# All four output-projection chunks ahead of the MLP: moving a half's norm and operand sums beside other matrix products

## The chip, the cores and the metric

The kernel runs on 1 core of one Trainium2 chip. The metric is the device time of one execution in microseconds; before the change it is 2526.63 us (median of 3 runs, 2519.16 to 2531.45). Five engines work side by side, each in the order of its own instruction queue: TensorE (PE; its weight loads are shown as PEld), VectorE (DVE), ScalarE (ACT), GpSimd (POOL) and SyncE (SP), which here only issues transfers.

## The reference

One decoder layer on 2048 tokens of width 1024, in float32. The normalised input goes through one combined projection into three head groups (a convolution, a retention and a dilated attention). Their outputs are joined into `mix`. What the change touches is all that follows:

```
mix = concatenate([conv_out, ret_out, att_out], axis=-1) @ w_out     # 1024 x 1024
x   = x + mix
h2  = rms_norm(x, norm2_g)
ff  = square(relu(h2 @ w_ff1)) @ w_ff2                               # 1024 -> 4096 -> 1024
out = x + ff
```

## The kernel before

Everything after attention is held transposed: 128 channels on the partitions, tokens along the free axis. The 2048 tokens are worked in two halves H of 1024, each half in two chunks c of 512. Chunks are written (H,c) here: (0,0), (0,1), (1,0), (1,1). Every float32 operand is split in two parts that TensorE takes: a rounded one (a copy on ACT) and the rest (a subtraction on DVE); `halves` (L616) does both. A product then takes three matmuls per 128 x 128 block (`mm3`, L915).

For each half the stages come one after the other:

1. Output projection. For both chunks and each of 8 blocks d of 128 output channels: load and split a weight block (`woraw`, `wohi`, `wolo`, L636), 24 matmuls into one bank `psc`, add the residual on DVE (L976), store the sum to DRAM from POOL's queue (L977), square it on ACT, add the squares into `ssum` on POOL (L983). In the last four blocks of a chunk the `mix` tiles of the next one are loaded and split. Weights and mix tiles come through the pool `stage`, which has 3 buffers; split weights lie in `wcp`, room for 3 blocks.
2. Norm and sums. `norm_sums` (4 small products `pm`), a power on POOL, `norm_rows` (4 small products `pr`), then the multiplications by `pr`. The up projection takes seven products of 512 x 512 x 128 where eight would be plain, on sums of the two chunks: B11 and B21 (from chunk 0 alone), T1, T2, T3, T4 and B22 (from both). `act_sums` (L1006) makes those sums from the 8 tiles `x1`, and `halves` splits them. Chunk 0 of a half is normalised beside the products of chunk 1; chunk 1 and the sums come after chunk 1's last product.
3. Up projection. 16 pairs of 128 hidden channels, each seven products of 12 matmuls (banks `psx`, `psy`, `psz`). Since the sums are late, the first FIRST = 3 pairs begin with the two products that need only B11 and B21.
4. Down projection. 8 groups g of 4 hidden blocks: load hidden rows and weights, split, 192 matmuls into `pso`, add into `acc` on DVE. In half 0's last group, half 1's first `mix` tiles are loaded; its output projection follows.

The order on each engine is made by a scheduler that simulates the program from its order in the source and from the buffers that are free; the pool `ur` has 24 buffers of 4 KB per partition, for operands and for hidden rows, `ul` 8 and `actp` 8.

Of the kernel before, what the change touches and what calls it, by code (L numbers as in the profile page):

```python
# [48 lines left out]
def kernel(ctx, tc, x, xT, w_in, g1, g2, conv_w, conv_b, conv_g, ret_g, qk_g,  # L49
# [871 lines left out]

    for H in range(2):

        x1 = []
        ssum = [tp.tile([P, CH], F32, tag="ssum", name=f"ssum{c}") for c in range(2)]
        ops = {}

        def norm_sums(c):
            pm = bank("pm2")
            for q in range(4):  # L930
                mm = nc.tensor.matmul(pm[:, q:q + 1], ssum[c][:, q * P:(q + 1) * P], ones[:], start=True, stop=True)
            ms = small.tile([P, 4], F32, tag="ms4", name="ms4")
            nc.vector.tensor_scalar(out=ms[:], in0=pm[:, 0:4], scalar1=1.0 / D, scalar2=EPS,
                                    op0=ALU.mult, op1=ALU.add)
            r2 = small.tile([P, 4], F32, tag="r2", name="r2")
            rsqrt(r2[:], ms[:], 4)
            return r2, mm

        def norm_rows(r2):
            pr = bank("pr2")  # L940
            for q in range(4):
                mm = nc.tensor.matmul(pr[:, q * P:(q + 1) * P], r2[:, q:q + 1].to_broadcast([P, P]), ident[:],
                                      start=True, stop=True)
            return pr, mm

        def after(ins):
            return tc.issue_after(ins.ins) if ins is not None else nullcontext()

        def op_b(name, kp, raw):
            u = unit4(ul, "v", name) if name in ("T1", "T4") else unit4(ur, "u", name)  # L950
            halves(raw, u)
            ops[name, kp] = u

        def load_mix1(k):
            u = unit4(ur, "u", f"mix{k}")
            raw = stage.tile([P, CH], F32, tag="raw", name="mixraw")
            nc.sync.dma_start(out=raw[:], in_=mix_d[k][H][:, CH:2 * CH])
            halves(raw[:], u)
            return u

        for d in range(KT):
            xt = unit4(ur, "u", f"x1_{d}", F32)
            nc.sync.dma_start(out=xt[:], in_=xT[d * P:(d + 1) * P, H * HALF:(H + 1) * HALF]
                              .rearrange("p (c t) -> p c t", c=2))
            x1.append(xt)
        mixes = [mix0 + [load_mix(7, 0, 0, actp)], []] if H == 0 else [mix0, []]
        for c in range(2):
            cs = slice(c * CH, (c + 1) * CH)
            mix = mixes[c]
            for d in range(KT):  # L970
                wo = wout0[d] if H == 0 and c == 0 and d < len(wout0) else load_wout(d)
                xt = x1[d]
                ps = bank("psc")
                for k in range(KT):
                    mm3(ps[:], (wo[0][:, k, :], wo[1][:, k, :]), hl(mix[k]), k == 0, k == KT - 1)
                nc.vector.tensor_tensor(out=xt[:, c, :], in0=xt[:, c, :], in1=ps[:], op=ALU.add)  # L976
                nc.gpsimd.dma_start(out=x1_d[d][:, cs], in_=xt[:, c, :])  # L977
                if d == 0:
                    nc.scalar.activation(out=ssum[c][:], in_=xt[:, c, :], func=AF.Square)
                else:  # L980
                    sq = tp.tile([P, CH], F32, tag="sq", name="sq2", bufs=1)
                    nc.scalar.activation(out=sq[:], in_=xt[:, c, :], func=AF.Square)
                    nc.gpsimd.tensor_tensor(out=ssum[c][:], in0=ssum[c][:], in1=sq[:], op=ALU.add)  # L983
                if H == 0 and c == 0 and d == LATE:
                    while todo:
                        tick()
                    late.close()
                    ul = ctx.enter_context(tc.tile_pool(name="ul", bufs=LAST, reuse_waits="tile"))
                if c == 0 and d >= 4:
                    mixes[1] += [load_mix1(2 * d - 8), load_mix1(2 * d - 7)]  # L990
                if c == 1:
                    nc.scalar.activation(out=xt[:, 1, :], in_=xt[:, 1, :], func=AF.Copy, scale=g2t[:, d:d + 1])
                if c == 1 and d == 1:
                    pr = norm_rows(norm_sums(0)[0])[0]
                    for k in range(KT):
                        nc.vector.scalar_tensor_tensor(out=x1[k][:, 0, :], in0=x1[k][:, 0, :], scalar=g2t[:, k:k + 1],
                                                       in1=pr[:], op0=ALU.mult, op1=ALU.mult)
                    for kp in range(4):
                        op_b("B11", kp, x1[kp][:, 0, :])
                        op_b("B21", kp, x1[kp + 4][:, 0, :])  # L1000
# [224 lines left out]
```

## Time and profile before

| | |
|---|---|
| median of 3 runs | 2526.63 us |
| profiled execution | 2526.32 us, span 2524.5 us |
| PE busy | 2451.7 us, 97% of the span |
| DVE, ACT, POOL busy | 59%, 35%, 21% |
| mean granted clock | 0.978 |

The span runs from the first to the last instruction. Busy shares are means over stages that differ; "granted clock" is the share of full speed that TensorE was given, and its two levels are 1.2 and 2.4 GHz. A window of the trace counts an instruction that crosses its edge on both sides. Half 0's output projection begins at 921.8 us, half 1's ends at 1825.5 us.

### The profile page before, as it was taken

Reading aid. Unit: us, or ns where it says so; the run is one execution under the profiler, and the core shown is the slowest. Engines: PE = TensorE matmul, PEld = TensorE weight load, DVE = VectorE, ACT = ScalarE, POOL = GpSimd, SP = SyncE. Lnnn points to the kernel's source line nnn. Section 1 sums busy time; section 2 is a strip of 40 time slices with the busy share of each in tenths; the row PEclk is TensorE's granted clock in tenths of the full one; section 3 lists DMA queues with packets and bytes.
Section 4 is the critical chain, followed back from the end, with each engine's and each line's share of the span. In section 5 each row is a group of like instructions: output and inputs, shape, how many; then the busy total and the mean of one; then the engine's idle time right before and its main releaser. Section 6 shows DMA issues by size and latency. Waiting matters only on the chain.

```text
span 2524.5 us, 32832 instructions
## 1 busy us (share of the span) xinstructions
PE 2451.7 (97%) x12062; PEld 2027.7 (80%) x12062; DVE 1483.5 (59%) x2864; ACT 884.9 (35%) x2005; POOL 537.9 (21%) x387
## 2 busy tenths in 40 slices
PE   7999999999999989899999999999989999999999
PEld 6878889999878767668888888888768888888887
DVE  5576787763486765785556545444586556654542
ACT  6433325333566564432223212112432223221210
POOL 0231212232142323642320000001553222000000
PEclk9999999999898899989999999999989999999999
DMA  7312104432353437222236323245422223632311
GB/s 222 122 63 72 43 14 118 114 95 81 101 114 76 106 103 255 88 100 109 100 111 224 132 79 122 67 160 181 143 73 110 109 109 119 222 122 71 117 67 67
DMA packets 189997, 284.19 MB, mean 113 GB/s; under 512 B 40093, under 2 KB 129292, under 8 KB 189836
## 3 DMA queue, kind: packets, MB, share of 16 engines
q1 hardware_dynamic: 187276, 273.70, 33.6%
q0 software_dynamic: 2560, 8.39, 0.9%
q8 instruction: 95, 1.56, 0.3%
q14 instruction: 66, 0.54, 0.1%
HBM read 210.04 MB, written 71.99 MB: 112 GB/s over the span
## 4 chain that ended last, share of the span: by engine, by line
PE 84%; DVE 6%; DMA 6%; ACT 2%; issue 1%; SPq 1%; POOL 0%; ACTq 0%; DVEq 0%; POOLq 0%
PE pso L917 28%; PE ps L158 15%; PE psy L917 11%; PE psz L917 7%; PE psx L917 6%; PE psc L917 5%; PE po L712 2%; PE pt L691 2%; PE sp L665 2%; DMA xn<-x 2%; PE sp L666 2%; DVE T L619 1%; PE rsp L350 1%; DMA woraw<-w_out 1%; PE rpo L365 1%
## 5 line engine op out<-in xcount | busy, mean ns | idle before, releaser
L917 PE MATMUL pso<-hid,w2a 128*128 128x512 f32 x1536 | 361.3, 396 | 0.0
L917 PE MATMUL pso<-hid,w2b 128*128 128x512 f32 x1536 | 361.0, 396 | 0.0
L1004 DVE TENSOR_TENSOR acc<-acc,pso 128x512 f32<-128x512 f32 x256 | 175.2, 685 | 296.0 <-PE pso L917 295.2
L917 PEld LDWEIGHTS pso<-hid,w2b 128*128 128x128 f32 x1536 | 288.6, 188 | 69.8
L917 PEld LDWEIGHTS pso<-hid,w2a 128*128 128x128 f32 x1536 | 288.6, 188 | 69.8
L158 PE MATMUL ps<-whi,hh 128*128 128x384 f32 (+1 forms) x896 | 313.5, 351 | 13.6 <-ACT whi L117 9.6
L158 PE MATMUL ps<-whi,hl 128*128 128x384 f32 (+1 forms) x896 | 315.0, 352 | 0.0
L158 PE MATMUL ps<-wlo,hh 128*128 128x384 f32 (+1 forms) x896 | 311.8, 348 | 0.0
L917 PE MATMUL psy<-T,S 128*128 128x512 f32 x768 | 203.3, 412 | 7.8 <-DVE T L619 5.5
L917 PE MATMUL psx<-B,A 128*128 128x512 f32 x768 | 191.2, 396 | 0.0
L158 PEld LDWEIGHTS ps<-whi,hh 128*128 128x128 f32 x896 | 169.5, 189 | 25.4 <-ACT whi L117 9.6
L917 PEld LDWEIGHTS psy<-T,S 128*128 128x128 f32 x768 | 149.6, 196 | 49.3 <-DVE T L619 10.3
L158 PEld LDWEIGHTS ps<-whi,hl 128*128 128x128 f32 x896 | 169.3, 189 | 11.3 <-issue 5.4
L158 PEld LDWEIGHTS ps<-wlo,hh 128*128 128x128 f32 x896 | 169.3, 189 | 9.6 <-issue 3.1
L217 DVE SCALAR_TENSOR_TENSOR acc<-cbuf,cwt,acc 128x512 f32<-128x512 f32 x240 | 175.5, 776 | 0.2
L917 PEld LDWEIGHTS psx<-B,A 128*128 128x128 f32 x768 | 144.0, 188 | 34.3
L1004 POOL TENSOR_TENSOR s<-w1raw 128x512 f32<-128x512 f32 x64 | 91.0, 1439 | 354.9 <-DMA w1raw<-w_ff 318.9
L917 PE MATMUL psc<-mix,wohi 128*128 128x512 f32 x512 | 163.1, 398 | 3.0 <-DVE ml L673 2.1
L619 DVE TENSOR_TENSOR S<-s,S 128x512 fp32r<-128x512 f32 x128 | 107.4, 843 | 68.8 <-ACT S L617 68.2
L676 ACT ACTIVATE lt<-lt,ml 128x256 f32<-128x256 f32 (+1 forms) x288 | 129.3, 452 | 29.9 <-DVE ml L673 29.3
L617 ACT ACTIVATE S<-s 128x512 fp32r<-128x512 f32 x128 | 80.0, 628 | 157.7 <-PE psy L917 94.1
L617 ACT ACTIVATE w2b<-w2raw 128x512 fp32r<-128x512 f32 x64 | 40.1, 626 | 260.2 <-DVE acc L1004 233.0
(192 smaller groups left out, 4011.8 us busy)
## 6 DMA issues: line engine op xcount, KB each, us to landing
w1raw<-w_ff SPq DMA_DIRECT2D x68, 512.0 KB, 3.3
hidraw<-hid_d SPq DMA_DIRECT2D x64, 512.0 KB, 4.2
w2raw<-w_ff SPq DMA_DIRECT2D x64, 512.0 KB, 4.0
woraw<-w_out SPq DMA_DIRECT2D x33, 512.0 KB, 4.0
hid_d<-hidB SPq DMA_DIRECT2D x32, 512.0 KB, 2.6
hid_d<-hidA SPq DMA_DIRECT2D x32, 512.0 KB, 2.6
xs<-xT SPq DMA_DIRECT2D x31, 512.0 KB, 3.9
qkraw<-qkT_d SPq DMA_DIRECT2D x48, 256.0 KB, 4.8
```

Of the source, the lines that this page charges most:

```text
L158: nc.tensor.matmul(ps, a[:, k, :], b[k][:], start=(k == 0 and m == 0), stop=(k == KT - 1 and m == 2))
L217: nc.vector.scalar_tensor_tensor(out=accs[j], in0=src, scalar=cwt[:, j, w:w + 1], in1=accs[j], op0=ALU.mult, op1=ALU.add)
L350: nc.tensor.matmul(sp[:, :w], kT[0:n, a, :], qm[0:n, h0:h1, :], start=True, stop=True)
L617: nc.scalar.activation(out=u[:, 0, :], in_=raw, func=AF.Copy)
L619: sub.tensor_tensor(out=u[:, 1, :], in0=raw, in1=u[:, 0, :].bitcast(F32), op=ALU.subtract)
L665: nc.tensor.matmul(sp[:, c0:c0 + n], qs[h][:, qsl], khi[h][:, ksl], start=True, stop=False)
L666: nc.tensor.matmul(sp[:, c0:c0 + n], qs[h][:, qsl], klo[h][:, ksl], start=False, stop=True)
L676: last_exp[0] = nc.scalar.activation(out=lt[:, :n], in_=lt[:, :n], func=AF.Exp, scale=-1.0, bias=mls[u][:, h:h + 1], accum_out=mls[u][:, 2 ...
L691: nc.tensor.transpose(pts[u][:, q * P:(q + 1) * P], lts[h, u][:, c * P:(c + 1) * P], ident[:])
L712: nc.tensor.matmul(po[h * 64:(h + 1) * 64, u0 * P:(u0 + n) * P], vt[:, kv, h * 64:(h + 1) * 64], mv, start=(one or i == 0), stop=(one or i ...
L917: nc.tensor.matmul(ps, w[a], act[b], start=(first and m == 0), stop=(last and m == 2), skip_group_check=more)
L1004: eng.tensor_tensor(out=out, in0=a, in1=b, op=op)
```

## The change

`out_chunk(H, c, mix, steps)` is now a function, and it runs four times, for (0,0), (0,1), (1,0) and (1,1), ahead of the first up projection. `steps` gives what the source places behind a block d. Norm and sums of half 0 stand beside the chunks of half 1. The residual sums of half 1 pass through 8 rotating tiles of `ul`, are stored to DRAM, and are loaded again into `x1` in half 0's down projection (group 5, block 7); their norm, left operands and sums stand beside half 0's last two groups or behind them. All sums and norm multiplications of chunk 1 are on DVE (12 operations per half were on POOL), the ACT scaling by g2 is gone, and FIRST is 2. The seven products, the down projection and the number of matmuls are as before.

```diff
-FIRST = 3
+FIRST = 2
+    def act_sums(H, kp):
+        lo, hi = x1[H, kp], x1[H, kp + 4]
+        tt(nc.vector, lo[:, 0, :], lo[:, 1, :], lo[:, 0, :], ALU.subtract)
+        t = ur.tile([P, CH], F32, tag="u", name="t2")
+        tt(nc.vector, t[:], hi[:, 1, :], lo[:, 0, :], ALU.subtract)
+        op_b("T2", kp, t[:])
+        tt(nc.vector, lo[:, 1, :], hi[:, 1, :], lo[:, 1, :], ALU.subtract)
+        tt(nc.vector, hi[:, 0, :], hi[:, 0, :], t[:], ALU.subtract)
...
+    def out_chunk(H, c, mix, steps):
+        cs = slice(c * CH, (c + 1) * CH)
+        for d in range(KT):
+            wo = wout0[d] if H == 0 and c == 0 and d < len(wout0) else load_wout(d)
+            if H == 0:
+                xt = x1[0, d][:, c, :]
+            else:
+                xt = ul.tile([P, CH], F32, tag="v", name="x1")
+                nc.sync.dma_start(out=xt[:], in_=xT[d * P:(d + 1) * P, HALF + c * CH:HALF + (c + 1) * CH])
+                xt = xt[:]
+            ps = bank("psc")
+            for k in range(KT):
+                mm3(ps[:], (wo[0][:, k, :], wo[1][:, k, :]), hl(mix[k]), k == 0, k == KT - 1)
+            tt(nc.vector, xt, xt, ps[:], ALU.add)
+            nc.gpsimd.dma_start(out=x1_d[H][d][:, cs], in_=xt)
...
+            for step in steps.get(d, ()):
+                step()
...
+    out_chunk(0, 1, mixes[1], {1: [lambda: norm_sums(0, 0)], 2: [lambda: normalise(0, 0)],
+                               **{d: [more(2, 2 * d - 8, ur), more(2, 2 * d - 7, ur)] for d in range(4, 8)}})
+    out_chunk(1, 0, mixes[2], {0: [lambda: norm_sums(0, 1)], 1: [lambda: normalise(0, 1)], 3: [lambda: left_ops(0)],
+                               **{d: [more(3, 2 * d - 8, actp), more(3, 2 * d - 7, actp)] for d in range(4, 8)}})
+    out_chunk(1, 1, mixes[3], {0: [lambda: norm_sums(1, 0)], **{kp + 1: [lambda kp=kp: act_sums(0, kp)]
+                                                               for kp in range(4)},
+                               5: [lambda: right_ops(0, ("T3", "T1"))]})
+    right_ops(0, ("T4", "B22"))
...
+            if H == 0 and j == 0:
+                norm_sums(1, 1)
...
+        def load_next():
+            for d in range(KT):
+                x1[1, d] = unit4(ur, "u", f"x1_{d}", F32)
+                nc.sync.dma_start(out=x1[1, d][:], in_=x1_d[1][d][:].rearrange("p (c t) -> p c t", c=2))
...
+        next_half = {(end - 3, 7): [load_next], (end - 2, 1): [lambda: normalise(1, 0)],
+                     (end - 2, 4): [lambda: normalise(1, 1)], (end - 1, 0): [lambda: left_ops(1)]}
+        for g in range(end):
+            group(g)
+        if H == 0:
+            sums_next()
+            right_ops(1, ("T3", "T1", "T4", "B22"))
```

How this moves instructions is seen at three places. First PE's queue from half 0's last output-projection block into the up projection, before (a row is one 128 x 512 block with its count; `psx` takes the products with B11 and B21, `pm` and `pr` are the small products of the norm):

```order
L917 MATMUL psx<-B_10525,A_10766 128x512 x3
L931 MATMUL pm_10782<-ones,ssum_9988 128x1 x4
L917 MATMUL psx<-B_10507,A_10796 128x512 x3
L917 MATMUL psx<-B_10513,A_10796 128x512 x3
L917 MATMUL psx<-B_10519,A_10796 128x512 x3
L917 MATMUL psx<-B_10525,A_10796 128x512 x3
L917 MATMUL psx<-B_10510,A_10812 128x512 x3
L917 MATMUL psx<-B_10516,A_10812 128x512 x3
L917 MATMUL psx<-B_10522,A_10812 128x512 x3
L917 MATMUL psx<-B_10528,A_10812 128x512 x3
L942 MATMUL pr_10828<-ident,r_10789 128x128 x4
L917 MATMUL psx<-B_10507,A_10928 128x512 x3
```

and now, behind the last block of chunk (1,1):

```order
L917 MATMUL psc<-mix_11152,wolo 128x512
L917 MATMUL psx<-B_10941,A_11561 128x512 x3
L917 MATMUL psx<-B_10947,A_11561 128x512 x3
L917 MATMUL psx<-B_10953,A_11561 128x512 x3
L917 MATMUL psx<-B_10959,A_11561 128x512 x3
L917 MATMUL psx<-B_10941,A_11582 128x512 x3
L917 MATMUL psx<-B_10947,A_11582 128x512 x3
L917 MATMUL psx<-B_10953,A_11582 128x512 x3
L917 MATMUL psx<-B_10959,A_11582 128x512 x3
L917 MATMUL psy<-T_11243,S_11631 128x512 x3
L917 MATMUL psy<-T_11289,S_11631 128x512 x3
L917 MATMUL psy<-T_11335,S_11631 128x512 x3
```

The norm's small products have left this place, and the first product on a sum (T2, tiles T_11243 and on, into `psy`) follows two products with B11.

Second, DVE's queue behind block 1 of half 1's first chunk, before (`wolo` is the rest part of a weight block, `mix` that of a mix tile, `x<-x,psc` the residual add):

```order
L976 TENSOR_TENSOR x_1_15337<-x_1_15337,psc 128x512
L642 TENSOR_TENSOR wolo<-woraw,wohi 128x1024
L619 TENSOR_TENSOR mix_15575<-mixraw,mix_15575 128x512
L619 TENSOR_TENSOR mix_15580<-mixraw,mix_15580 128x512
L976 TENSOR_TENSOR x_2_15339<-x_2_15339,psc 128x512
L642 TENSOR_TENSOR wolo<-woraw,wohi 128x1024
L619 TENSOR_TENSOR mix_15621<-mixraw,mix_15621 128x512
L619 TENSOR_TENSOR mix_15626<-mixraw,mix_15626 128x512
L976 TENSOR_TENSOR x_3_15341<-x_3_15341,psc 128x512
```

and now, from the weight split behind that block's residual add on:

```order
L642 TENSOR_TENSOR wolo<-woraw,wohi 128x1024
L619 TENSOR_TENSOR mix_11051<-mixraw,mix_11051 128x512
L950 SCALAR_TENSOR_TENSOR x_0_9996<-x_0_9996,g2t,pr_10852 128x512
L950 SCALAR_TENSOR_TENSOR x_1_9998<-x_1_9998,g2t,pr_10852 128x512
L950 SCALAR_TENSOR_TENSOR x_2_10000<-x_2_10000,g2t,pr_10852 128x512
```

then four more of the eight multiplications with `pr`, and the rest of the rows up to the next weight split:

```order
L950 SCALAR_TENSOR_TENSOR x_7_10010<-x_7_10010,g2t,pr_10852 128x512
L929 TENSOR_TENSOR x_0_9996<-x_0_9996 128x512
L619 TENSOR_TENSOR mix_11056<-mixraw,mix_11056 128x512
L929 TENSOR_TENSOR x_1_9998<-x_1_9998 128x512
L929 TENSOR_TENSOR x_2_10000<-x_2_10000 128x512
L929 TENSOR_TENSOR x_10871<-x_10871,psc 128x512
L929 TENSOR_TENSOR x_3_10002<-x_3_10002 128x512
L642 TENSOR_TENSOR wolo<-woraw,wohi 128x1024
```

Half 0's second norm and the first subtractions of its sums have come between two weight splits of half 1.

Third, DVE's queue where half 1's sums are made, before (behind the half's last output-projection block):

```order
L1004 TENSOR_TENSOR x_0_15335<-x_0_15335,pr_16092 128x512
L1004 TENSOR_TENSOR x_1_15337<-x_1_15337,pr_16092 128x512
L1004 TENSOR_TENSOR x_2_15339<-x_2_15339,pr_16092 128x512
L1004 TENSOR_TENSOR x_3_15341<-x_3_15341,pr_16092 128x512
L1004 TENSOR_TENSOR x_0_15335<-x_0_15335 128x512
L1004 TENSOR_TENSOR x_1_15337<-x_1_15337 128x512
L1004 TENSOR_TENSOR x_2_15339<-x_2_15339 128x512
L1004 TENSOR_TENSOR x_3_15341<-x_3_15341 128x512
L619 TENSOR_TENSOR A_16290<-w1raw,A_16290 128x512
L1004 TENSOR_TENSOR t_16111<-x_4_15343,x_0_15335 128x512
L619 TENSOR_TENSOR T_16151<-x_0_15335,T_16151 128x512
```

and now, in the last group of half 0's down projection (acc_13668 is its block d = 7, added to once per chunk):

```order
L929 TENSOR_TENSOR acc_13666<-acc_13666,pso 128x512 x2
L929 TENSOR_TENSOR t_16057<-x_4_15378,x_0_15370 128x512
L929 TENSOR_TENSOR x_4_15378<-x_4_15378,t_16057 128x512
L929 TENSOR_TENSOR t_16065<-x_5_15380,x_1_15372 128x512
L619 TENSOR_TENSOR T_16059<-t_16057,T_16059 128x512
L929 TENSOR_TENSOR acc_13668<-acc_13668,pso 128x512
L929 TENSOR_TENSOR x_5_15380<-x_5_15380,t_16065 128x512
L619 TENSOR_TENSOR T_16112<-x_4_15378,T_16112 128x512
```

The differences between the two chunks and the splits of T1 now stand ahead of these rows, beside the last group's products; the tiles `t` and T of T2 come when that group's hidden rows free their buffers.

## Rows read from the trace of the kernel before

**Rows 1.** Page part 1, busy us (share of the span) xinstructions; page part 2, granted clock in 40 slices.

```profile
PE 2451.7 (97%) x12062; PEld 2027.7 (80%) x12062; DVE 1483.5 (59%) x2864; ACT 884.9 (35%) x2005; POOL 537.9 (21%) x387
...
PEclk9999999999898899989999999999989999999999
```

**Rows 2.** Windows: us, busy by engine (xinstructions), PEclk, DMA share, GB/s.

```profile
1040.00:1060.00 20.00, 18.21 (x87) 14.73 (x86) 10.63 (x15) 10.18 (x19) 8.78 (x7) 1.00 0.21 77
1060.00:1080.00 20.00, 12.18 (x29) 7.07 (x28) 20.00 (x16) 5.89 (x11) 16.88 (x12) 0.64 0.09 27
1080.00:1100.00 20.00, 16.37 (x56) 11.88 (x55) 18.79 (x25) 8.66 (x16) 8.15 (x5) 0.76 0.17 53
1200.00:1300.00 100.00, 100.00 (x433) 81.03 (x432) 56.31 (x72) 28.03 (x48) 29.96 (x23) 1.00 0.29 106
1840.00:1860.00 20.00, 12.77 (x41) 8.35 (x39) 20.00 (x16) 6.40 (x11) 18.04 (x11) 0.77 0.08 26
```

**Rows 3.** Timeline of PE, first transition: start us, us, instruction, count, [idle before <-releaser].

```profile
1040.60 0.40 PE L917 MATMUL psc<-mix,wolo 128*128 128x512 f32 x1
...
1045.59 1.05 PE L931 MATMUL pm<-ones,ssum 128*128 128x1 f32 x8 [1.79 <-POOL ssum L983]
...
1052.18 1.05 PE L942 MATMUL pr<-ident,r 128*128 128x128 f32 x8
1052.99 8.64 PE L917 MATMUL psx<-B,A 128*128 128x512 f32 x36
...
1067.40 1.65 PE L917 MATMUL psz<-T,S 128*128 128x512 f32 x3 [5.53 <-DVE T L619]
...
1101.92 3.43 PE L917 MATMUL psy<-T,S 128*128 128x512 f32 x14
```

**Rows 4.** Timeline of PE, second transition.

```profile
1825.53 0.40 PE L917 MATMUL psc<-mix,wolo 128*128 128x512 f32 x1
...
1886.56 3.66 PE L917 MATMUL psy<-T,S 128*128 128x512 f32 x15
```

**Rows 5.** Timeline of DVE, first transition.

```profile
1070.64 0.68 DVE L619 TENSOR_TENSOR T<-x,T 128x512 fp32r<-128x512 f32 x1
1071.24 1.76 DVE L1004 TENSOR_TENSOR t<-x,x 128x512 f32<-128x512 f32 x1
```

**Rows 6.** Timeline of POOL, first transition.

```profile
1044.28 1.25 POOL L983 TENSOR_TENSOR ssum<-ssum,sq 128x512 f32<-128x512 f32 x1 [0.24 <-ACT sq L982]
...
1060.04 6.75 POOL L1004 TENSOR_TENSOR x<-x,x 128x512 f32<-128x512 f32 x4
```

**Rows 7.** DVE by form, half 0 down and half 1 output projection: busy us, mean ns.

```profile
L1004 DVE TENSOR_TENSOR acc<-acc,pso 128x512 f32<-128x512 f32 x128 | 87.6, 684 | 140.4 <-PE pso L917 140.0
...
L642 DVE TENSOR_TENSOR wolo<-woraw,wohi 128x1024 fp32r<-128x1024 f32 x16 | 20.1, 1254 | 3.4 <-ACT wohi L641 3.4
...
L996 DVE SCALAR_TENSOR_TENSOR x<-x,g2t,pr 128x512 f32<-128x512 f32 x8 | 5.3, 740 | 0.0
```

**Rows 8.** Timeline of SP, half 1 output projection: its transfers in order.

```profile
1744.25 0.33 SPq L638 DMA_DIRECT2D woraw<-w_out  x1
...
1764.65 28.41 SPq L638 DMA_DIRECT2D woraw<-w_out  x8
```

**Rows 9.** Page part 6, transfers: count, KB each, median us to landing.

```profile
woraw<-w_out SPq DMA_DIRECT2D x33, 512.0 KB, 4.0
```

**Rows 10.** Windows, the end of attention.

```profile
965.00:970.00 5.00, 5.00 (x22) 3.61 (x21) 2.51 (x5) 0.00 (x0) 4.18 (x4) 1.00 1.03 414
```

**Rows 11.** Timeline of SP, half 0 output projection.

```profile
980.39 0.33 SPq L638 DMA_DIRECT2D woraw<-w_out  x1
...
987.17 20.96 SPq L638 DMA_DIRECT2D woraw<-w_out  x8
```

**Rows 12.** Timeline of PE, half 0 output projection.

```profile
993.37 0.73 PE L917 MATMUL psc<-mix,wohi 128*128 128x512 f32 x2 [0.87 <-ACT wohi L641]
```

**Rows 13.** Tile hidraw, half 0 down projection: count, ns min/median/max, first and last start.

```profile
L619 DVE TENSOR_TENSOR hid<-hidraw,hid x64: 682/685/694, 1347.4 to 1658.3; 128x512 fp32r<-128x512 f32 x64
```

More of the change, by code (lines that the diff above doesn't have):

```diff
@@ L920 @@
     hl = lambda u, cs=slice(None): (u[:, 0, cs], u[:, 1, cs])
-    for H in range(2):
[L924 to L1000, printed above, removed]
-        def tt(eng, out, a, b, op):
-            eng.tensor_tensor(out=out, in0=a, in1=b, op=op)
-        def act_sums(pr):
-            rs = tp.tile([P, CH], F32, tag="sq", name="rs", bufs=1)
-            nc.scalar.activation(out=rs[:], in_=pr[:], func=AF.Copy)
-            for kp in range(4):
-                lo, hi = x1[kp], x1[kp + 4]
-                tt(nc.vector, lo[:, 1, :], lo[:, 1, :], pr[:], ALU.mult)
-                tt(nc.gpsimd, hi[:, 1, :], hi[:, 1, :], rs[:], ALU.mult)
-                tt(nc.vector, lo[:, 0, :], lo[:, 1, :], lo[:, 0, :], ALU.subtract)
-            for kp in range(4):
-                lo, hi = x1[kp], x1[kp + 4]
-                t = ur.tile([P, CH], F32, tag="u", name="t2")
-                tt(nc.vector, t[:], hi[:, 1, :], lo[:, 0, :], ALU.subtract)
-                op_b("T2", kp, t[:])
-                tt(nc.gpsimd, lo[:, 1, :], hi[:, 1, :], lo[:, 1, :], ALU.subtract)
-                tt(nc.gpsimd, hi[:, 0, :], hi[:, 0, :], t[:], ALU.subtract)
-            for name, h, c in (("T3", 0, 1), ("T1", 0, 0), ("T4", 4, 0), ("B22", 4, 1)):
-                for kp in range(4):
-                    op_b(name, kp, x1[kp + h][:, c, :])
@@ new lines, with tt, norm_sums @@
+    rn = const.tile([P, NT], F32, name="rn")
+    ops = {}
+    x1 = {}
+    ssums = {}
+    def tt(eng, out, a, b, op):
+        eng.tensor_tensor(out=out, in0=a, in1=b, op=op)
+    def norm_sums(H, c):
+        ssum = ssums.pop((H, c))
+        pm = bank("pm2")
+        for q in range(4):
+            nc.tensor.matmul(pm[:, q:q + 1], ssum[:, q * P:(q + 1) * P], ones[:], start=True, stop=True)
+        ms = small.tile([P, 4], F32, tag="ms4", name="ms4")
+        nc.vector.tensor_scalar(out=ms[:], in0=pm[:, 0:4], scalar1=1.0 / D, scalar2=EPS,
+                                op0=ALU.mult, op1=ALU.add)
+        n = (2 * H + c) * 4
+        rsqrt(rn[:, n:n + 4], ms[:], 4)
@@ new lines, in right_ops, with load_mixed @@
+    def right_ops(H, names):
+        for name, h, c in (("T3", 0, 1), ("T1", 0, 0), ("T4", 4, 0), ("B22", 4, 1)):
+            if name in names:
+                for kp in range(4):
+                    op_b(name, kp, x1[H, kp + h][:, c, :])
+    def load_mixed(H, c, k, pool):
+        u = unit4(pool, "act" if pool is actp else "u", f"mix{k}")
+        raw = stage.tile([P, CH], F32, tag="raw", name="mixraw")
+        nc.sync.dma_start(out=raw[:], in_=mix_d[k][H][:, c * CH:(c + 1) * CH])
+        halves(raw[:], u)
+        return u
@@ L1044, in first_half @@
             a11 = op_a("A11", ra[:, 0, :])
-            with after(behind):
-                product(xb[:], a11, "B11", True, True)
+            product(xb[:], a11, "B11", True, True)
             nc.scalar.activation(out=et[:, 0, :], in_=xb[:], func=AF.Copy)
```

65 lines of the change are left out of this document (52 added, 13 removed).

## The prediction

> **What bounds the kernel now.** I read the page's busy shares first: TensorE is busy for 97% of the span, so only its idle time and its slow clock are left to win, and DVE, ACT and POOL matter where they make it wait [rows 1]. The row of granted clocks over 40 slices is 9 nearly everywhere. Next I went through the span in windows and looked for those in which PE is not full or the clock is below 1.00. Behind the output projections there are two such places, the same one in each half: around 1060 to 1100 us, and around 1840 to 1880 us [rows 2]. In steady work 433 instructions take 100 us, 0.231 us each; in the 20 us from 1060 on there are 29. The granted clock is 0.64 and 0.76 there, between the two levels of 1.2 and 2.4 GHz, after PE had waited.
>
> Third, the timeline of PE between the last product of the output projection and the point where it runs steadily again, 1040.60 to 1101.92 us [rows 3]. The names of the releasers tell the story: POOL's `ssum` (1.79 us), then several times DVE's T, 5.53 us the longest. The last matmul before and the first behind the second place are 1825.53 and 1886.56 [rows 4]. Fourth, what DVE does in that time: it makes the sums, and an operation on 128 x 512 that takes 0.68 us alone takes 1.76 where one of POOL's runs beside it (6.75 us for four of those) [rows 5, 6].
>
> **What is removed.** The first stretch is 61.32 us long, the second 61.03 [rows 3, 4]. By the queue each holds 157 matmuls of 512 columns, and the 8 + 8 small ones `pm` and `pr`. At 0.231 us each (steady work), or (8.64 - 0.40 + 0.24) / 36 = 0.236 (the 36 from 1052.99 on [rows 3]), 157 take 36.3 to 37.0 us; I take 36.6. The small ones are 1.05 us twice, and are only moved. So 61.3 - 36.6 - 2.1 = 22.6 us and 22.3 us are lost, **45 us together**. That is the most the change can give here: the matmuls are the same before and after. Part of it is waiting and part the slow clock, but the slow clock follows the waiting (after the idle 1.79 us at 1045 the window still has 1.00, after the 5.53 us it does not [rows 2]), so both go or stay together.
>
> **What comes in its place, term by term.**
>
> *Half 0's norm and sums beside half 1's chunks, chunk (1,0): 5 us, from 0 to 12.* A block of 24 matmuls takes 24 x 0.233 = 5.6 us of PE. In the last four blocks of a chunk the weight block and two mix tiles of the next chunk share the 3 buffers of `stage`, and there the kernel before issued its weights from 1744.25 to 1764.65 in three steps, 6.8 us each [rows 8]: slower than PE eats, covered by up to three blocks of split weights. Now that cover is used up, since DVE gets half 0's second norm just then. Counted from the start of (1,0): the split of block 4 ends near 14.3 us; its buffer is then free, the next loads land 4.0 us later [rows 9], the mix tile is split at 19.8; the rows behind it are eight multiplications at 0.74, six operations at 0.68 (the residual add among them) and the split at 1.25 [rows 7], 11.2 us. Block 5's weights are there at about 31.0, and PE, which is through block 4 at 29.4 (two short norm products included), is 1.6 us late. The three blocks behind have some 0.7 us more on DVE than the 6.8 us, so about 7.5 against 5.6, which the wider flow around them leaves at about 1 us late each. POOL's eight `ssum` adds of 1.25 us [rows 6] slow a few of these splits; 5 us in all. The end at 0 is the queue before, where PE did not wait at all; the end at 12 is 3 us for each of four blocks.
>
> *Chunk (0,1): 1 us, 0 to 3.* Same pattern, with half 0's first norm in DVE's queue, but the blocks start with the full cover; I find block 7 ready 1 to 2 us ahead of its use.
>
> *The crowded start: 1.5 us, 0 to 5.* The first eight residual tiles of half 1, 8 x 256 KB = 2.1 MB, stand in SP's queue among the weights of (0,0)'s last blocks, and SP issues them as soon as `ul` has memory. The weights there were issued 6.8 us apart, at 980.39 and 987.17 [rows 11], and PE waited for the next one at 993.37 [rows 12], so each us of delay is a us of PE. In this stage 414 GB/s have been moved in 5 us [rows 10]; 2.1 MB at that rate are 5 us, the upper end; most of it lies in gaps between the weights, so 1.5.
> The Trainium skill (DMA: Bandwidth & Descriptors, section Where 436 GB/s comes from) says that an HBM transfer is bound by the memory's share of about 358 GB/s per core. By an estimate from that page the same 2.1 MB would be 6 us and this term about 2; the trace does not agree, since it shows 414, so the row stands.
>
> *Half 0's start of the up projection: 1 us, 0 to 3.* T2, T3, T1 and B22 are split before the last output product; only three of the four T4 tiles, the weights' parts and POOL's four sums of w1 are left, against 24 matmuls (5.6 us) that need only B11.
>
> *Half 1's start: 4.5 us, 0.5 to 9.* The last group's hidden rows hold 8 of `ur`'s 24 buffers, so the T2 tiles wait for its last block. From the first add of that block to the split of S for the second pair DVE has 31 operations at 0.68 = 21.1 us, starting 2.8 us before PE is through: 18.3, and some 1.5 of waiting for buffers. PE needs that operand after 84 matmuls, at 19.6: just in time. But POOL's four sums for the second pair fall into this time, 6.75 / 4 = 1.7 us each [rows 6], and each makes one DVE operation 1.08 us longer (1.76 for 0.68 [rows 5]), 4.3 us together. I take 4.5; the lower end is without that, the upper if each of the 8 products in front waits 0.5 more and 4.5 stay.
> The Trainium skill (SBUF — State Buffer, section Who interferes with whom) says that a DVE instruction with two SBUF inputs and a GpSimd one that reads SBUF exclude each other for a whole instruction. The trace agrees [rows 5, 6]. By that rule taking 12 operations from POOL helps DVE more than it costs it, 12 x (1.08 - 0.68) = 4.8 us a half; without it, moving them would cost DVE 8.2 us a half.
>
> *At nothing:* the reload of half 1's sums (4 MB) and its norm run beside the down projection, where the last hidden tile was split at 1658.3 [rows 13], while the last group begins near 1825.5 - 16 x 5.6 - 44 = 1692. With x1 in place 16 buffers are left for hidden rows, two groups, and 34 us of lead are more than the 8 loads of 512 KB at 4 us in sequence. FIRST = 2 costs nothing if the sums are on time; the scaling by g2 on ACT was never late.
>
> **Sum.** 45 - (5 + 1 + 1.5 + 1 + 4.5) = 32 us. The profiled execution took 2526.32 us (span 2524.5), and the median is 2526.63, so either base serves: 2526.3 - 32 = **2494 us**. With all terms at their low ends the gain is 44.5, with all at their high ends 13: 2482 to 2513. Likely 2486 to 2504.
>
> **Rivals.**
> 1. *Everything is hidden* (gain 40 or more, about 2483). For it: DVE is busy 59% of the span, and the chunks have room on average. Against it: `stage` with three buffers already ran at 6.8 us a block.
> 2. *One half's gap stays* (gain 13 to 22, about 2508). If half 1's T2 tiles get their buffers late, PE waits over 5 us again at that place and its clock falls, as at 1067, some 14 us more than my terms: 2526 - 45 + 13 + 14. Against it: chunk differences and T1 are made ahead.
> 3. *No change* (within 0.5%, 12.6 us, which is about what can be told from no change here). The gap moves into the output projection: half 0's norm, sums and splits are 44 operations at 0.68 and 16 at 0.74, 42 us of DVE, and if three quarters of it (31) delayed weight splits, 45 - 31 - 8 = 6 us would be left: 2520. Against it: up to three blocks are split in advance, so only DVE time beyond 5.6 us a block counts.
> 4. *Slower.* The weight chain through `stage` decides: load 4.0, the ACT copy, the split 1.25 and what stands before them in both queues, with one weight in flight for each block. In the eight last blocks of (0,1) and (1,0) it must take 5.6 us to cost nothing; from 5.6 + 45 / 8 = 11.2 us a block it eats the whole gain; at 13 us it costs 8 x 7.4 = 59 and ends at 2526 - 45 + 59 + 7 = 2547. For it: the new rows between two splits are 11.2 us once. Against it: that long row occurs once, not eight times.
>
> **How the numbers follow.** Forecast (gain 22 to 40) 0.60; rival 1 0.14; rival 2 0.15; rival 3 0.06; rival 4 0.05. Faster by over 0.5% is the first three, 0.89; same 0.06; slower 0.05. The range reaches from the low ends less the spread of the runs (2482 - 3) into rival 2: 2479 to 2510.
>
> **What would show it.** After the change no stretch behind the output projections should have a clock below 0.9, and PE's waits on T should be under 2 us each. Waits on `wolo` or `wohi` should appear in chunk (1,0), blocks 5 to 8, about 5 us; a few on T or S at half 1's first pairs. In half 1's region the time from half 0's last `pso` product to the first `psx` should be under 1 us. The forecast is wrong if PE waits over 10 us for `wolo`, if hidden rows are late in half 0's last two groups, or if the attention part ahead of 920 us, whose order is the same, changes.

## The result and the profile after

The changed kernel takes 2487.49 us (median of 4 runs, 2485.31 to 2490.92), the one before 2522.89 beside it (4 runs, 2518.83 to 2531.45): ratio 0.9857, 95% interval 0.9824 to 0.9889. That is 35.4 us less; forecast were 32 and 2494, range 2479 to 2510. The profiled execution took 2485.31 us, span 2483.5.

Runs of one kernel differ by up to 20 us. As far as the profiles show, most of that lies in the attention part, whose instruction order no edit here touches: in the fourteen profiles of this study the first output product starts anywhere from 907.3 to 930.6 us. So the profiles are compared from that product on, cut at marks that PE's timeline shows: the small products of chunk (0,1)'s sums (`pm`), the first `psx` product of half 0, that of half 1, and the end of the span. From the first output product to the end it is 1602.7 us before and 1565.1 after, **37.6 us less**. The last stretch, from half 1's first `psx` product, went from 698.7 to 675.5; of these 23.2 us 2.1 are small products that now run earlier, and 21.1 are the gap. The two starts, before and after:

```profile
1825.76 2.96 PE L917 MATMUL psx<-B,A 128*128 128x512 f32 x12
1807.95 2.26 PE L917 MATMUL psx<-B,A 128*128 128x512 f32 x9
```

Some 2 us of the 37.6 are not the change (an estimate): over the 60 us from the first output product the granted clock was 0.94 before and 0.98 after.

The page, as in [rows 1]:

```profile
PE 2434.3 (98%) x12062; PEld 2019.5 (81%) x12062; DVE 1478.2 (60%) x2888; ACT 873.0 (35%) x1987; POOL 504.1 (20%) x363
...
PEclk9999999999898999999999999999999999999999
```

The windows of the two former gaps and of steady work, as in [rows 2]. The first three lie in the output projection now, the last two hold half 1's start (first `psx` at 1807.95):

```profile
1060.00:1080.00 20.00, 20.00 (x87) 16.11 (x86) 15.82 (x20) 7.69 (x11) 9.65 (x8) 1.00 0.65 217
1080.00:1100.00 20.00, 16.58 (x69) 13.54 (x69) 18.65 (x28) 11.34 (x18) 9.77 (x6) 0.88 0.51 178
1100.00:1120.00 20.00, 20.00 (x86) 16.40 (x85) 11.89 (x13) 8.71 (x12) 8.32 (x8) 0.95 0.47 157
1200.00:1300.00 100.00, 100.00 (x432) 80.86 (x431) 59.18 (x75) 27.55 (x47) 27.18 (x20) 1.00 0.32 117
1800.00:1820.00 20.00, 20.00 (x87) 16.10 (x86) 17.84 (x30) 13.32 (x25) 5.02 (x1) 1.00 0.37 132
1820.00:1840.00 20.00, 19.37 (x84) 15.10 (x83) 12.70 (x19) 5.36 (x11) 13.88 (x8) 1.00 0.16 52
```

Both gaps are gone. All that PE still waits for from 975 us on (engine, line, releaser: us in total, times, longest):

```profile
PE pm L935 <- POOL ssum L929: 3.4, 1, 3.4
PE psc L917 <- ACT wohi L641: 2.7, 2, 1.6
PE psc L917 <- DVE wolo L642: 1.0, 2, 0.5
PE psy L917 <- DVE S L619: 0.5, 1, 0.5
```

The second and third line are the crowded start, 3.77 us against 2.27 before, where the same view has

```profile
PE psc L917 <- DVE wolo L642: 1.4, 2, 0.9
PE psc L917 <- ACT wohi L641: 0.9, 1, 0.9
```

The fourth line of the view after is half 1's start. The first, the wait on `ssum`, was in no term of the prediction. PE's timeline at that wait, in chunk (1,1); the `pm` products belong to chunk (1,0):

```profile
1092.44 0.39 PE L917 MATMUL psc<-mix,wolo 128*128 128x512 f32 x1
1096.24 1.87 PE L935 MATMUL pm<-ones,ssum 128*128 128x1 f32 x8 [3.42 <-POOL ssum L929]
1097.97 1.20 PE L917 MATMUL psc<-mix,wohi 128*128 128x512 f32 x2
```

POOL's timeline, the add that it waits for and the one before (1.25 us in [rows 6]):

```profile
1083.16 1.79 POOL L929 TENSOR_TENSOR ssum<-ssum,sq 128x512 f32<-128x512 f32 x1 [1.68 <-ACT sq L1005]
1089.41 0.56 POOL L999 DMA_DIRECT2D x_d<-x  x1 [4.46 <-DVE x L929]
1089.98 6.21 POOL L929 TENSOR_TENSOR ssum<-ssum,sq 128x512 f32<-128x512 f32 x1
```

And DVE's, beside the end of that add:

```profile
1093.79 1.27 DVE L619 TENSOR_TENSOR T<-x,T 128x512 fp32r<-128x512 f32 x2
1094.99 0.67 DVE L929 TENSOR_TENSOR x<-x,psc 128x512 f32<-128x512 f32 x1
1095.59 1.15 DVE L619 TENSOR_TENSOR T<-x,T 128x512 fp32r<-128x512 f32 x1
```

From 1089.6 on DVE has no gap: differences and splits of half 0 and a weight split, two SBUF inputs each. POOL's add ends at 1096.19; take off the 1.25 us of an undisturbed one, and it seems to have got going at 1094.94, when DVE began the residual add, the one operation in the row behind the add's start with an operand from PSUM. The next DVE operation then took 1.15 us instead of 0.68. The kernel before already shows this, in rows that the prediction did not read and at a place where nobody waits for the add: it took 4.33 us, and its last 1.25 begin at 1025.95, with a residual add:

```profile
1022.87 4.33 POOL L983 TENSOR_TENSOR ssum<-ssum,sq 128x512 f32<-128x512 f32 x1 [1.32 <-ACT sq L982]
```

```profile
1025.96 0.68 DVE L976 TENSOR_TENSOR x<-x,psc 128x512 f32<-128x512 f32 x1
1026.56 1.72 DVE L642 TENSOR_TENSOR wolo<-woraw,wohi 128x1024 fp32r<-128x1024 f32 x1
```

At half 1's start POOL stands again, here in its sums of w1, while DVE goes on at 0.68 each; of the two sums the first took 9.57 us, to the end of DVE's row, and the second 1.28:

```profile
1814.98 10.82 POOL L929 TENSOR_TENSOR s<-w1raw 128x512 f32<-128x512 f32 x2 [38.52 <-DVE S L619]
```

### The profile page after: what moved, and what is told of

Its sections match the earlier page's. It is cut to its first block, busy times and chain, and to the rows that moved or that the text cites. A ratio compares the mean times of both kernels' runs of the same rounds, so it can differ in the third digit from the quotient of the medians.

```text
span 2483.5 us, 32837 instructions
## 1 busy us (share of the span) xinstructions
PE 2434.3 (98%) x12062; PEld 2019.5 (81%) x12062; DVE 1478.2 (60%) x2888; ACT 873.0 (35%) x1987; POOL 504.1 (20%) x363
## 3 DMA queue, kind: packets, MB, share of 16 engines
q1 hardware_dynamic: 189292, 276.85, 34.9%
## 4 chain that ended last, share of the span: by engine, by line
PE 88%; DVE 5%; DMA 3%; ACT 1%; issue 1%; POOL 1%; SPq 0%; ACTq 0%; DVEq 0%; POOLq 0%
PE pso L917 29%; PE ps L158 16%; PE psy L917 11%; PE psz L917 7%; PE psx L917 7%; PE psc L917 6%; PE po L712 2%; PE sp L665 2%; PE pt L691 2%; PE sp L666 2%; DMA xn<-x 1%; PE rsp L350 1%; PE rpo L365 1%; DMA xs<-xT 1%; PE pb L167 1%
## 5 line engine op out<-in xcount | busy, mean ns | idle before, releaser
L917 PE MATMUL psy<-T,S 128*128 128x512 f32 x768 | 192.4, 396 | 0.6 <-DVE S L619 0.5
L917 PEld LDWEIGHTS psy<-T,S 128*128 128x128 f32 x768 | 143.9, 188 | 36.2 <-DVE S L619 1.0
L676 ACT ACTIVATE lt<-lt,ml 128x256 f32<-128x256 f32 (+1 forms) x288 | 129.2, 452 | 28.8 <-DVE ml L673 28.2
L617 ACT ACTIVATE hid<-hidraw 128x512 fp32r<-128x512 f32 x128 | 74.3, 626 | 164.6 <-DMA hidraw<-hid_d 116.2
```

Of the source, the lines that this page charges most:

```text
L617: nc.scalar.activation(out=u[:, 0, :], in_=raw, func=AF.Copy)
L676: last_exp[0] = nc.scalar.activation(out=lt[:, :n], in_=lt[:, :n], func=AF.Exp, scale=-1.0, bias=mls[u][:, h:h + 1], accum_out=mls[u][:, 2 ...
L917: nc.tensor.matmul(ps, w[a], act[b], start=(first and m == 0), stop=(last and m == 2), skip_group_check=more)
```

## The experiments

Us from the profiles, by the marks above ("to pm": chunk (0,1)'s small products; "to up 0", "to up 1": first `psx` of a half), and medians with the ratio to the kernel before. Stretches and sums are right to about 0.1 us:

| kernel | output, to pm | to up 0 | to up 1 | to end | sum | median | ratio, interval |
|---|---|---|---|---|---|---|---|
| changed | 127.3 | 89.1 | 673.2 | 675.5 | 1565.1 | 2487.5 | 0.986 (0.982-0.989) |
| 1 sums later | 132.2 | 82.6 | 673.2 | 675.5 | 1563.5 | 2480.2 | 0.983 (0.981-0.985) |
| 2 add on DVE | 129.5 | 82.6 | 673.2 | 675.6 | 1561.0 | 2478.6 | 0.983 (0.981-0.985) |
| 3 sums on POOL | 130.5 | 89.2 | 673.2 | 676.5 | 1569.4 | 2493.0 | 0.987 (0.985-0.989) |
| 4 norm in open | 128.5 | 89.0 | 673.1 | 686.4 | 1577.0 | 2495.6 | 0.989 (0.988-0.991) |
| 5 x later | 127.2 | 90.1 | 673.2 | 675.6 | 1566.1 | 2490.8 | 0.988 (0.985-0.992) |
| 6 norm twice | 129.5 | 87.3 | 673.2 | 675.6 | 1565.7 | 2481.1 | 0.984 (0.980-0.988) |
| 7 half 0 behind | 130.4 | 87.0 | 673.2 | 675.9 | 1566.6 | 2489.6 | 0.987 (0.983-0.990) |
| 8 both (1 and 5) | 125.6 | 82.7 | 674.4 | 675.6 | 1558.2 | 2477.2 | 0.984 (0.981-0.987) |
| 9 norm 0 behind | 131.7 | 82.6 | 692.4 | 675.6 | 1582.4 | 2502.4 | 0.992 (0.989-0.995) |
| 10 open, POOL | 132.0 | 88.8 | 673.1 | 692.8 | 1586.7 | 2503.8 | 0.993 (0.990-0.995) |
| 11 both open | 129.2 | 82.6 | 691.9 | 692.8 | 1596.4 | 2518.3 | 0.998 (0.996-1.000) |
| 12 one input | 125.3 | 83.4 | 673.2 | 675.5 | 1557.5 | 2483.3 | 0.984 (0.980-0.987) |

A stretch that an edit doesn't reach agrees to 0.4 us, the first excepted (the crowded start and the slow clock ahead of it): effects of a few us are read from the stretches, not the medians.

**1, sums later**

```
- out_chunk(1, 1, ..., {0: [norm_sums(1, 0)], ...})
+ out_chunk(1, 1, ..., {..., 6: [norm_sums(1, 0)]})
```

> The four small products of half 1's first chunk, which wait for POOL's ssum in the last chunk of the output projection, are issued six blocks later; all else stays. Theory S (POOL's last ssum add is held up by DVE's unbroken row of half 0's sums, 6.21 us for 1.3, and TensorE has to stand for it): the wait of 3.4 us and the slow clock behind it (together 6 us) are gone, the stretch from the first output product to the end goes from 1565 to 1559 us, the median to about 2481; POOL's add still takes 5 us or more, only nobody waits for it. Rival W (the weights' way through the stage is what is late in these chunks, and the wait on ssum only hides it): a wait on wohi or wolo of 2 to 6 us comes in its place, the time stays within 2 us.

Theory S holds: the wait is gone, nothing takes its place, "to up 0" is 6.5 us shorter. POOL's add is as slow as before:

```profile
1092.47 6.23 POOL L929 TENSOR_TENSOR ssum<-ssum,sq 128x512 f32<-128x512 f32 x1
```

**2, the last add on DVE**

```
- tt(nc.gpsimd, ssums[H, c], ssums[H, c], sq, ALU.add)
+ eng = nc.vector if (H, c, d) == (1, 0, KT - 1) else nc.gpsimd
+ tt(eng, ssums[H, c], ssums[H, c], sq, ALU.add)
```

> One instruction changes its engine: the last ssum add of half 1's first chunk runs on DVE instead of POOL. Theory S: it takes 0.7 us instead of 6.2, TensorE's wait on ssum falls under 0.5 us, the stretch from the first output product to the end is about 1559 us (5 to 6 less). Rival L (not POOL's add but the late residual add, 4 us behind its product in DVE's queue, decides): the wait stays above 2 us, time within 2 us.

The add takes 0.67 us and the wait is gone, again 6.5 us. The `pm` products were also placed some 2 us further back in PE's queue, less than the 3.4 of the wait: POOL's add was what was late.

```profile
1092.42 0.67 DVE L929 TENSOR_TENSOR ssum<-ssum,sq 128x512 f32<-128x512 f32 x1
```

**3, half 1's sums on POOL** (both operations were on `nc.vector`)

```
+ eng = nc.gpsimd if H == 1 else nc.vector
+ tt(eng, lo[:, 1, :], hi[:, 1, :], lo[:, 1, :], ALU.subtract)
+ tt(eng, hi[:, 0, :], hi[:, 0, :], t[:], ALU.subtract)
```

> Of half 1's sums 8 operations of 128 x 512 (lo1 and hi0) run on POOL, as in the kernel before; half 0 keeps all on DVE. Theory S (DVE's row holds POOL off): POOL's operations take 3 to 6 us each while DVE works through its row, T3 and T4 come late, TensorE waits over 5 us at half 1's start and its clock falls: 10 to 25 us longer. The prediction's term (each POOL operation delays one DVE operation by 1.08 us and saves it 0.68): 8 x 0.4 = 3.2 us more on DVE, 1 to 4 us longer. Rival N: it lies beside other work, within 1 us.

1.0 us longer at half 1: my price for S was wrong, and between the prediction's term (1 to 4) and rival N (within 1) this does not decide. The operations were placed beside the last two groups, where DVE has gaps, and took 1.3 to 1.7 us. POOL's next two, beside the unbroken row, took 9.12:

```profile
1807.27 1.62 POOL L929 TENSOR_TENSOR x<-x,t 128x512 f32<-128x512 f32 x1 [1.90 <-DVE t L929]
1812.95 9.12 POOL L929 TENSOR_TENSOR s<-w1raw 128x512 f32<-128x512 f32 x2 [4.06 <-DMA w1raw<-w_ff]
```

**4, half 1's second norm in the open**

```
- (end - 2, 4): [normalise(1, 1)]
+ behind the last group: normalise(1, 1), then sums_next(), right_ops(1, ...)
```

> The norm of half 1's second chunk (8 multiplications on DVE and 8 small products) is made behind the last group of the down projection, as the kernel before does it behind its output projection; the differences and splits follow. Theory J (half 1's start is just in time, its 0.5 us of wait has no slack in front): 8 x 0.7 + 1 = 6.5 us later, TensorE waits 5 to 8 us on T or S and the clock falls: 9 to 15 us longer than the changed kernel, about 2497 to 2502. Rival K (slack of several us): under 4 us. If a half's whole gap came from the norm, 22 us longer.

10.9 us more, as theory J has it: half 1's start is just in time. The window of that start, and POOL's timeline in it: while DVE is full, one of POOL's sums is under way all the time.

```profile
1820.00:1840.00 20.00, 13.57 (x38) 8.12 (x39) 20.00 (x34) 11.58 (x22) 14.63 (x1) 0.83 0.14 53
```

```profile
1825.37 19.82 POOL L929 TENSOR_TENSOR s<-w1raw 128x512 f32<-128x512 f32 x2 [7.17 <-DVE S L619]
1845.14 1.75 POOL L929 TENSOR_TENSOR s<-s,w1raw 128x512 f32<-128x512 f32 x1
```

**5, residual tiles later** (the edit in short)

```
+ nc.scalar.activation(out=xt[:, 0:1], in_=x1[0, d][:, 1, 0:1], func=AF.Copy)
  nc.sync.dma_start(out=xt[:], in_=xT[...])      # issued behind block d of chunk (0,1)
```

> The eight residual tiles of half 1's first chunk (2.1 MB) no longer stand among the last weights of chunk (0,0): each is loaded behind the residual add of the same block of chunk (0,1), by a write of one column on ACT ahead of it; the second chunk's tiles are unchanged. Theory D (these loads delay the weights, 1.5 us in the prediction; the profiles of the changed kernel and its variants show waits on wohi and wolo of 3.7 to 4.6 us there, the kernel before 2.3): the waits fall back to 2.0 to 2.5 us, the stretch from the first output product to the small products of chunk (0,1)'s sums gets 1.5 to 2 us shorter, more where the clock fell there. Rival G (the weights are late for the stage's buffers, not for the memory): the waits stay at 3.5 to 4.5.

Theory D: the waits fall to 0.88 + 0.86 + 0.53 = 2.27 us, those of the kernel before (the middle one is [rows 12]). The first two:

```profile
995.73 0.50 PE L917 MATMUL psc<-mix,wolo 128*128 128x512 f32 x1 [0.88 <-DVE wolo L642]
...
1001.87 0.73 PE L917 MATMUL psc<-mix,wohi 128*128 128x512 f32 x2 [0.86 <-ACT wohi L641]
```

The stretch as a whole did not get shorter than the changed kernel's in this one profile (127.2): over the 60 us from the first output product the clock was 0.94 here and 0.98 there, which hides the 1.5 us. The nine profiles with the crowd that also had 0.94 there took 128.5 to 132.1. Behind it the wait on `ssum` was 4.0 us instead of 3.4, and "to up 0" 1.0 longer.

**6, the norm twice**

```
+ if (H, c) == (0, 1):
+     nc.vector.scalar_tensor_tensor(out=xc, in0=xc, scalar=1.0, in1=xc, op0=ALU.mult, op1=ALU.max)
```

> In chunk (1,0) eight more DVE operations of 128 x 512 (each a maximum of a tile with itself, values unchanged) stand behind the eight norm multiplications of half 0's second chunk: 8 x 0.68 = 5.4 us more in the row between two weight splits. Theory C (the splits are two to three blocks ahead there, at the narrowest 9.7 us, so the row is covered): no wait on wohi or wolo in the chunks of half 1, the weights' lead shrinks by 4 to 6 us, the time changes by less than 2 us. The prediction's reading (the cover is used up at blocks 5 to 8): TensorE waits 5 to 10 us on wolo there.

Theory C was wrong: PE waits 2.1 us for weights at the start of (1,1), and "to up 0" is 4.7 us over the 82.6 of the runs without a wait (the `pm` products were placed later here, so their wait is absent); behind the wait the clock fell (0.91 from 1080 to 1100 us). By 5.4 us more on DVE and 2.1 of wait some 3.3 us of cover are left in the changed kernel. Its own trace has 4.2 at the narrowest, at the first block of (1,1): the split ended at 1080.03, PE first used it at 1084.27. The 9.7 of the expectation is not there.

```profile
1090.32 0.73 PE L917 MATMUL psc<-mix,wohi 128*128 128x512 f32 x2 [1.59 <-ACT wohi L641]
1091.59 0.50 PE L917 MATMUL psc<-mix,wolo 128*128 128x512 f32 x1 [0.54 <-DVE wolo L642]
```

**7, half 0's sums behind**

```
  out_chunk(1, 1, mixes[3], {0: [norm_sums(1, 0)]})
+ for kp in range(4): act_sums(0, kp)
+ right_ops(0, ("T3", "T1", "T4", "B22"))
```

> Half 0's sums (the 16 differences and the splits of T1 to T4 and B22) are made behind the last block of the output projection instead of beside it; norm, B11, B21 and half 1's part stay early. Theory P (the whole gain is DVE work taken out of the open): 16 x 0.68 + 20 x 0.68 = 24 us of DVE row stand against 24 to 48 products that are ready (5.6 to 11 us), so TensorE waits 8 to 14 us on T and S, the clock falls: 12 to 20 us longer from the first product of the up projection to half 1's first, and the wait on ssum in chunk (1,1) is gone, since DVE's row no longer holds POOL off (6 us less): about 6 to 14 us longer in all. Rival Q (the early norm alone brings the gain): within 3 us of the changed kernel.

It undid nothing: the scheduler starts a DVE operation when its inputs are ready, so the first difference for T2 ran 35.1 us behind the `pm` products of chunk (0,1)'s sums (34.9 in the changed kernel), still in chunk (1,0), and POOL's last add took 5.60 us. Neither theory is tested. A place in the source holds work back where it needs a product of PE's: experiment 9 moves the norm's small products, and the norm moves with them.

**8, both**

```
+ the edits of 1 and of 5
```

> The sums of half 1's first chunk read six blocks later, as in the first experiment, and the residual tiles loaded later, as above. Theories S and D together: 6.4 and 1.5 to 2 us less than the changed kernel, no wait of more than 2.5 us left behind the attention part; median about 2479, the best of all. If one of the two only moves the wait, 2 to 6 us less.

1558.2 us from the first output product, 6.9 less than the changed kernel; the median, 2477.21, is the lowest, but its interval overlaps that of the changed kernel. Half 0's start costs 1.1 us more there (PE waits for S).

**9, half 0's second norm behind**

```
- out_chunk(1, 0, ..., 1: [normalise(0, 1)], ...)
+ behind out_chunk(1, 1): normalise(0, 1), act_sums(0, kp), right_ops(0, ...)
```

> Half 0's second norm (8 small products on TensorE, 8 multiplications on DVE), and with it the sums that need it, is made behind the last output product; TensorE issues its rows in the written order, so this time the sums can't move ahead. B11, B21 and all of half 1 stay as changed. Theory S: without DVE's row in the last chunk POOL's last ssum add takes 1.3 to 2 us and the wait on ssum there is gone (6.4 us less); at half 0's start 48 products (11 us) stand ready against the norm and the first sums, so the same 11 us come back that this cost at half 1: the stretch from chunk (0,1)'s small products to half 1's first product of the up projection gets 11 - 6.4, about 4 to 5 us longer. If POOL's add is slow for another reason, the wait of 3.4 us stays and it gets 11 longer; if half 0 has slack that half 1 has not, it gets 6 us shorter.

The first part of S holds: without the row POOL's last add of (1,0) takes 1.68 us, the wait is gone, "to up 0" 6.5 us shorter. The gap that comes back is 19.2 us, not 11, so the stretches from `pm` to half 1 get 12.7 us longer, not 4 to 5. POOL's timeline shows what the expectation left out: its 128 x 4 power operation, 1.03 us at its shortest, was held for 9.24, the w1 sums stood behind it, and PE waited for S (second fence); the clock fell to 0.63 (third, its window).

```profile
1096.33 1.68 POOL L929 TENSOR_TENSOR ssum<-ssum,sq 128x512 f32<-128x512 f32 x1
...
1149.86 9.24 POOL L81 TENSOR_TENSOR rn<-ms,power 128x4 f32<-128x4 f32 x1 [6.25 <-DVE ms L937]
```

```profile
1163.49 0.80 PE L917 MATMUL psy<-T,S 128*128 128x512 f32 x1 [7.28 <-ACT S L617]
```

```profile
1160.00:1180.00 20.00, 11.05 (x28) 7.85 (x29) 16.53 (x20) 9.85 (x18) 10.38 (x8) 0.63 0.07 26
```

**10, open and on POOL**

```
+ the edits of 3 and of 4
```

> As the fourth experiment (half 1's second norm behind the last group), and the 8 operations of half 1's sums that the kernel before had on POOL are there again. To be compared with the fourth: 686.4 us from half 1's first product of the up projection to the end of the span. Theory S (beside DVE's row POOL's operations take 3 to 6 us each, T3 and T4 wait for them): 5 to 10 us more, 692 to 697, near the 698.7 of the kernel before. The prediction's term (8 operations, 0.4 us of DVE each): 3 us more. Rival N: POOL only takes work from DVE, 3 to 5 us less.

6.4 us more than experiment 4, 17.3 more than the changed kernel: S. POOL's four differences took 14.95 us, the first 11.29 of them: its last 1.25 begin at 1832.8, when DVE's row ended (1832.94). Then DVE stood 9 us, since the next T needed them.

```profile
1822.78 14.95 POOL L929 TENSOR_TENSOR x<-x,x 128x512 f32<-128x512 f32 x4 [43.25 <-DVE x L929]
```

```profile
1832.26 0.68 DVE L619 TENSOR_TENSOR T<-t,T 128x512 fp32r<-128x512 f32 x1
1842.09 1.08 DVE L619 TENSOR_TENSOR T<-x,T 128x512 fp32r<-128x512 f32 x1 [9.15 <-ACT T L617]
```

**11, both halves open**

```
+ the edits of 9 and 10, half 0's 8 operations on POOL too
```

> Both of the above: in both halves the second norm and the sums stand behind the products in front of them, with 8 of the sums' operations on POOL, while the output projection of all four chunks still runs ahead of the MLP and half 1's sums still come back from DRAM. If the gain is the norm and the sums taken out of the open, and not the order of the chunks, 28 to 38 of the 37.6 us between the two profiles are lost again: 1595 to 1603 us from the first output product to the end of the span. If the order of the chunks itself brings a good part, 1575 to 1590.

1596.4 us: 31.3 of the 37.6 us are lost again, and the time is that of the kernel before within 0.4%, although the four chunks still run first. By stretches 18.7 + 17.3 = 36.0 come back, and 6.5 are saved on the `ssum` wait.

**12, one input**

```
+     nc.vector.tensor_scalar(out=xc, in0=xc, scalar1=1.0, scalar2=0.0, op0=ALU.mult, op1=ALU.add)
```

> As the sixth experiment, but the eight extra DVE operations in chunk (1,0) read one SBUF tile instead of two (times 1, plus 0; values unchanged). In the sixth, POOL's ssum add that starts as they begin took 5.21 us, in the changed kernel without them 2.80, and 1.28 beside an idle DVE. Theory S2 (only DVE operations with two SBUF inputs hold POOL off): it takes under 2.8 us, about 1.3 to 2.0, since POOL gets through beside them. Rival B (any unbroken row on DVE holds POOL off): 4.5 to 6 us again. The weights' lead shrinks as there or less: a wait of 0 to 2.5 us on wohi and wolo in chunk (1,1).

Not decided: POOL's add took 3.69 us, between the two. It met the last two of the extra operations (0.36 us each) for only 0.7 us; then came operations with two inputs, and it seems to have got in at the residual add, 1068.10. No wait for weights came in (1,1).

```profile
1065.66 3.69 POOL L929 TENSOR_TENSOR ssum<-ssum,sq 128x512 f32<-128x512 f32 x1 [1.23 <-ACT sq L1007]
```

```profile
1064.95 1.43 DVE L953 TENSOR_SCALAR x<-x 128x512 f32<-128x512 f32 x4
1066.29 1.89 DVE L929 TENSOR_TENSOR x<-x 128x512 f32<-128x512 f32 x3
1068.10 0.68 DVE L929 TENSOR_TENSOR x<-x,psc 128x512 f32<-128x512 f32 x1
1068.70 1.19 DVE L929 TENSOR_TENSOR x<-x 128x512 f32<-128x512 f32 x1
```

## Why the prediction was right

- **What is removed, 45 us: right.** Half 1's part was 21.1 us for 22.3 predicted. Half 0's follows by difference: from the first output product to half 1's first `psx` it was 903.9 us before and 889.6 after, 14.4 less; with half 1's small products (2.1), which lie there now, and the new waits below (6.5 and 1.5) that makes 24.5 for 22.6, the luck of the clock included. Opening both halves again brings 36.0 back. Waiting and slow clock left together.
- **Chunk (1,0), 5 us: no wait for weights.** The weights' way was the right thing to fear (5.4 us more on DVE brings the wait). The step that failed is the load and mix split that I counted ahead of the long row. From the start of (1,0), at 1037.23, the split of block 4 ended at 14.4 us (14.3 predicted), and the row took 10.1 us (11.2); but it began at 16.2, not at 19.8. The mix tile whose load followed block 4's split was itself split within the row, at 1059.32, and the load of block 5's weights was issued at 1046.44, before block 4's split. So block 5 was ready at 26.3 us for 31.0, 4.4 us ahead of its use (1067.93) instead of 1.6 late. DVE's timeline, both splits and parts of the row:

```profile
1050.38 1.23 DVE L642 TENSOR_TENSOR wolo<-woraw,wohi 128x1024 fp32r<-128x1024 f32 x1 [0.17 <-ACT wohi L641]
1052.76 0.69 DVE L619 TENSOR_TENSOR mix<-mixraw,mix 128x512 fp32r<-128x512 f32 x1 [1.16 <-ACT mix L617]
1053.44 5.36 DVE L950 SCALAR_TENSOR_TENSOR x<-x,g2t,pr 128x512 f32<-128x512 f32 x8
...
1059.32 0.68 DVE L619 TENSOR_TENSOR mix<-mixraw,mix 128x512 fp32r<-128x512 f32 x1
...
1062.32 1.22 DVE L642 TENSOR_TENSOR wolo<-woraw,wohi 128x1024 fp32r<-128x1024 f32 x1
```

- **The `ssum` wait in (1,1): in no term, 6.5 us** by experiments 1 and 2 (3.4 of wait, the rest slow clock behind it). The prediction priced POOL's `ssum` adds only by what they cost DVE; that one of them could itself come late, and PE stand for it, it put at nothing without a reason.
- **Chunk (0,1) 1 us, half 0's start 1 us: both 0.** Block 7 of (0,1) was ready 9.4 us ahead of its use, not 1 to 2.
- **The crowded start, 1.5 us: 1.5** (3.77 against 2.27), undone in experiment 5. The hit is in part luck: ten other profiles with the crowd have 3.0 to 5.8 us of such waits, 0.7 to 3.5 more than before.
- **Half 1's start, 4.5 us: 0.5.** The step that failed is that each of POOL's sums makes one DVE operation 1.08 us longer. That reading of [rows 5, 6] was taken where the two alternate; beside DVE's unbroken row it was POOL that stood (10.82 us for two), and DVE did not pay. Just in time was right: experiment 4 shows it.

So 6.5 + 1.5 + 0.5 = 8.5 us came in place of the 13, and 45 - 8.5 = 36.5, between the 35.4 of the medians and the 37.6 of the profiles. The forecast hit because two terms that came too high (5 and 4.5) outweighed one not seen, which is luck. Of the signs given, no waits on T, a dense start of both halves and under 1 us between the last `pso` and the first `psx` came true; waits for weights in (1,0) did not, and one window had 0.88. The attention part ahead, 3.4 us shorter in these two profiles, differs no more than between the others.

That the gain is the norm and the sums leaving the open, and not the order of the chunks by itself, is shown by experiment 11. It also puts 8 of each half's sums back on POOL. In half 1 that place makes 6.4 of its 17.3 us (experiment 10 against 4), though beside the last groups it costs 1.0 (experiment 3); in half 0 it makes nothing that shows (18.7 us with it, 19.2 without, experiment 9). Open is the rest: 6.3 us between experiment 11 and the kernel before, and 3.8 of half 1's 21.1. FIRST = 3, the other four operations per half on POOL and the scaling by g2 on ACT were not put back one by one, and the crowd and the early clock vary from run to run.

## What to carry to other kernels

Work that stands between two stages was worth its whole length here, and the slow clock behind it, once it ran beside products of another part; look then for what its dense row takes from others. In this kernel a small operation on POOL on the critical path did not belong beside a row of two-input DVE operations: on DVE, or with its result read later, it cost nothing. Moving a line in the code moves nothing if a scheduler orders by readiness (experiment 7); look at which instruction really holds the place.
